# Gates of a hybrid block: one 512-column and one 256-column product a block in place of three of 256, and shorter pauses in the RWKV chain

## The chip, the cores and the metric

The kernel runs on one core of a Trainium2 chip. The metric is the device time of one execution in microseconds. Before the change the median of three runs is 1736.51 us (1735.34 to 1737.04).

The core has a matrix engine (PE, which loads weights, PEld in the profile, beside its matmuls), a vector engine (DVE), a scalar engine (ACT), GpSimd (POOL) and SyncE (SP), which here only issues DMAs. Each works through its own queue in order and waits on semaphores.

## The reference

One layer over 256 tokens of width 2048, in float32. The part that matters here is the first half: a projection gives the gates and the inputs of four branches (RG-LRU, attention with forgetting, SSD, RWKV-7); each branch's output goes through a matrix of its own, is multiplied by its gate, and the four are added.

```python
xn = rmsnorm(h, mix_norm[i])
proj = jnp.einsum('bsd,dn->bsn', xn, w_in[i])
(g_raw, a_x, a_g, b_q, b_k, b_v, b_f, c_z, c_xbc, c_dt, d_u) = jnp.split(proj, _offsets(IN_SPLIT), axis=-1)
...
gates = jax.nn.sigmoid(g_raw.astype(jnp.float32)).reshape(Bsz, S, N_BRANCH, D)
merged = gates[:, :, 0] * jnp.einsum('bsc,cd->bsd', branches[0], w_branch[i, 0])
for j in range(1, N_BRANCH):
    merged = merged + gates[:, :, j] * jnp.einsum('bsc,cd->bsd', branches[j], w_branch[i, j])
h = h + jnp.einsum('bsd,de->bse', merged, w_out[i]).astype(h.dtype)
...
# at the end of the RWKV branch
mean = jnp.mean(y, axis=-1, keepdims=True)
var = jnp.mean(jnp.square(y - mean), axis=-1, keepdims=True)
y = (y - mean) * lax.rsqrt(var + RWKV_LN_EPS) * ln_w.reshape(H, N) + ln_b.reshape(H, N)
```

A feed-forward part (2048 to 2 x 5632 and back) and a gated embedding follow; the change does not touch them.

## The kernel before

**Split products.** The weights are float32, and PE multiplies float32r. So each weight chunk of 512 KB (four blocks of 128 rows by 256 columns) comes in by one DMA on SP's queue into `wr`; `split` makes a high part of it on ACT (`wh`, a cast, line 214) and a low part on DVE (`wl = wr - wh`, line 215). There are three buffers each of `wh` and `wl`. The activations x are split in the same way into tiles of 512 columns: 256 tokens of the high part, then 256 of the low part. Each block is then the sum of three products: wh with the high x, wh with the low x, and wl with the high x.

**Two forms of a block.** `product` (line 242) does a block in two matmuls: `wh` with all 512 columns of x, so that a bank of PSUM holds the two sums side by side, and `wl` with the high 256 columns. The two halves of the bank are added afterwards by `joined` (line 254): a copy on ACT (line 256) and an add on DVE. Where x is handed over as a pair of halves (`halves`, and the tuple branch of `gemm_fm`), a block is three matmuls of 256 columns, all into the same half of the bank, and no `joined` is needed. The gates (`gate_unit`, line 1163) and the branch outputs (`branch_unit`, line 1171) have the second form; nearly all other projections, `w_out`, `w_up` and `w_down` have the first.

**The gate stage.** It goes branch by branch: a, c, b, d. For each branch there are 8 gate units; a unit is 256 output columns, two tiles (`m`) of 128, with K = 2048 in 16 blocks, four chunks. For the first three branches a branch unit (K = 512, one chunk, 24 matmuls) follows each gate unit; for the last (d, RWKV) the eight gate units run first, then `ready(3, "d")`, then the eight branch units. Units take their two banks of PSUM in turn from `psG`, which has four (`pg` in the profile).

**The four branches' own work** is written as Python generators (`lru`, `fox`, `ssd`, `rwkv`). `gemm_fm` calls a hook, `pump` (line 1091), after each tile of each chunk, and `pump` advances the oldest active generator by a step. So a `yield` in the generator is a place where projection work comes between two steps; `yield n` skips n hook calls, a time for a DMA to land. The chain of RWKV is the last: a triangular inverse by a recursion of 31 steps over `prod` and Q (a product on DVE, then a reduction, line 929), a round trip of the inverse through DRAM (`rw_q`, read into `qat` and `qbd`), `yield 9`, two sets of small products, four chunks of state, then centring with a matrix (`center`, four steps), squares with a mask matrix (`selR`, four steps of two products into `pr`, eight rows), a reciprocal, a square root and Newton steps, a round trip of the norm through DRAM (`rw_gn`), and the last multiplications.

**What sets the order.** Instructions are recorded in three lanes of priority: "g" (loads, splits, evacuations), "b" (the branches) and "m" (the projections' matmuls). A scheduler places each engine's instructions by priority and by its own estimate of when they are ready; a matmul of a branch takes the place of the projection's matmuls of that moment plus 16 (`on_pe`, line 130). On the chip each engine then keeps that order.

## Time and profile before

| | us |
|---|---|
| median of three runs (1735.34 to 1737.04) | 1736.51 |
| profiled execution | 1736.75 |
| its span | 1735.0 |

The span is the time from the first to the last instruction that the profile of this execution holds. The gates' weights are issued from 280.3 to 764.8 us; the feed-forward part follows. Lines that name `pg<-x,wh` and `pg<-x,wl` are projections, `pg<-sb,wh` and `pg<-sb,wl` branch outputs, `pb<-...` the branches' own products. A row of a group gives line, engine, operation, tiles, shapes and count, then busy time and mean duration in ns, then the idle time of the engine ahead of it and what ended it. In a timeline the columns are start, duration, engine, line, operation, tiles, with the wait ahead in brackets. A reader can find the chain, the groups and the waits quoted with the prediction.

### The profile page before, as it was taken

The page shows a single profiled execution, that of the slowest core. Times are in us where ns is not written, and L with a number is a line of the kernel's source. Part 1 is how long each engine was busy: PE and PEld are TensorE (multiplying, and loading weights), DVE is VectorE, ACT ScalarE, POOL GpSimd, SP SyncE. Part 2 cuts the span into 40 slices and gives each one's busy share as a digit, 9 for nine tenths or more (in the row PEclk, how much of TensorE's full clock was granted, in tenths as well). Part 3 has the DMA queues.
Part 4 walks back from the last instruction along what each step waited for, and adds up shares of the span by engine and source line. Part 5 has one row for each costly group of instructions (what it writes and reads, how often), then busy time and mean ns, then how long its engine had stood idle before and what let it go on. Part 6 is the DMA issues. An engine that isn't in the chain of part 4 may idle for free.

```text
span 1735.0 us, 29610 instructions
## 1 busy us (share of the span) xinstructions
PE 1716.0 (99%) x11555; PEld 1559.9 (90%) x11555; DVE 1232.9 (71%) x2002; ACT 948.8 (55%) x1428; POOL 92.8 (5%) x155
## 2 busy tenths in 40 slices
PE   9999999999999999999999999999999999999998
PEld 7888888999999999999888888888888888888887
DVE  6888768687789744648778777777777755555666
ACT  6677545556644444545556555555555544444554
POOL 1000000002320100000110000000000000000000
PEclk9999999999999999999999999999999999999999
DMA  9556556557775744565766656666566666666564
GB/s 328 170 170 203 177 172 220 184 181 209 207 214 172 262 153 149 175 187 182 250 212 191 192 187 191 189 189 192 186 191 201 211 207 189 195 192 186 174 224 134
DMA packets 99132, 338.36 MB, mean 195 GB/s; under 512 B 12362, under 2 KB 16624, under 8 KB 98736
## 3 DMA queue, kind: packets, MB, share of 16 engines
q1 hardware_dynamic: 90528, 310.94, 57.6%
q0 software_dynamic: 7456, 21.81, 4.2%
q10 hardware_dynamic: 1008, 3.73, 0.5%
q8 instruction: 90, 1.47, 0.3%
q14 instruction: 50, 0.41, 0.1%
HBM read 326.95 MB, written 9.48 MB: 194 GB/s over the span
## 4 chain that ended last, share of the span: by engine, by line
PE 89%; issue 8%; DMA 1%; DVE 1%; ACT 0%; POOL 0%; SPq 0%; DVEq 0%; POOLq 0%
PE pg L132 85%; PE pb L135 3%; PE pb L132 1%; DMA e<-ssd_ac 0%; DMA d<-in_xT_dram 0%; DVE wl L215 0%; DMA wr<-in_w_ax_dram 0%; DVE s L100 0%; DVE e L116 0%; ACT wh L214 0%; DMA ssd_ac<-sb 0%; DVE e L929 0%; DVE e L100 0%; SPq L382 0%; POOL prm L415 0%
## 5 line engine op out<-in xcount | busy, mean ns | idle before, releaser
L132 PE MATMUL pg<-x,wh 128*128 128x512 f32 (+1 forms) x4384 | 1173.4, 340 | 5.5 <-DVE sb L100 5.3
L215 DVE TENSOR_TENSOR wl<-wr,wh 128x1024 fp32r<-128x1024 f32 (+1 forms) x592 | 715.8, 1210 | 407.3 <-ACT wh L214 398.9
L214 ACT CAST wh<-wr 128x1024 fp32r<-128x1024 f32 (+1 forms) x592 | 615.2, 1041 | 646.4 <-PE pg L132 500.5
L132 PE MATMUL pg<-x,wl 128*128 128x256 f32 (+1 forms) x3344 | 919.2, 282 | 5.4 <-DVE wl L215 5.2
L132 PEld LDWEIGHTS pg<-x,wh 128*128 128x128 f32 x4384 | 748.7, 188 | 91.7 <-issue 3.2
L132 PEld LDWEIGHTS pg<-x,wl 128*128 128x128 f32 (+1 forms) x3344 | 629.6, 189 | 19.8 <-DVE wl L215 7.9
L132 PE MATMUL pg<-f,wh 128*128 128x512 f32 x704 | 243.2, 390 | 0.0
L132 PE MATMUL pg<-f,wl 128*128 128x256 f32 x704 | 195.8, 282 | 0.0
L132 PEld LDWEIGHTS pg<-f,wh 128*128 128x128 f32 x704 | 131.7, 188 | 26.9
L132 PEld LDWEIGHTS pg<-f,wl 128*128 128x128 f32 x704 | 133.0, 189 | 1.0
L132 PE MATMUL pg<-sb,wh 128*128 128x256 f32 x512 | 94.7, 283 | 0.0
L120 DVE SCALAR_TENSOR_TENSOR s<-s,prm 128x255 f32<-128x255 f32 (+1 forms) x176 | 84.2, 479 | 1.7 <-ACT s L127 1.0
L132 PEld LDWEIGHTS pg<-sb,wh 128*128 128x128 f32 x512 | 79.2, 188 | 0.1
L256 ACT COPY s<-pg 128x256 f32<-128x256 f32 x136 | 49.7, 366 | 44.7 <-PE pg L132 44.7
L132 PE MATMUL pg<-sb,wl 128*128 128x256 f32 x256 | 72.4, 284 | 0.0
L100 DVE TENSOR_TENSOR s<-s 128x256 f32<-128x256 f32 (+1 forms) x172 | 70.5, 420 | 1.3
L127 ACT ACTIVATE s<-s 128x256 f32<-128x256 f32 x140 | 56.6, 412 | 15.4 <-DVE s L100 15.0
L100 DVE TENSOR_TENSOR s<-s,pg 128x256 f32<-128x256 f32 x136 | 56.3, 415 | 9.4 <-ACT s L256 8.1
L127 ACT ACTIVATE s<-s,prm 128x256 f32<-128x256 f32 x88 | 52.5, 596 | 0.7 <-DVE s L100 0.7
L127 ACT ACT_TABLE_LOAD x40 | 51.3, 1283 | 2.2 <-PEq L1375 1.2
L132 PEld LDWEIGHTS pg<-sb,wl 128*128 128x128 f32 x256 | 48.0, 188 | 0.2
L132 PE MATMUL pg<-d,wh 128*128 128x512 f32 x128 | 45.2, 395 | 0.0
(235 smaller groups left out, 1154.0 us busy)
## 6 DMA issues: line engine op xcount, KB each, us to landing
wr<-in_w_up_dram SPq DMA_DIRECT2D x176, 512.0 KB, 4.3
wr<-in_w_g_dram SPq DMA_DIRECT2D x128, 512.0 KB, 3.9
wr<-in_w_down_dram SPq DMA_DIRECT2D x88, 512.0 KB, 4.3
wr<-in_w_p_dram SPq DMA_DIRECT2D x76, 512.0 KB, 3.8
wr<-in_w_branch_dram SPq DMA_DIRECT2D x32, 512.0 KB, 4.2
wr<-in_w_out_dram SPq DMA_DIRECT2D x32, 512.0 KB, 3.9
wr<-in_w_ple_gate_dram SPq DMA_DIRECT2D x32, 512.0 KB, 4.7
wr<-in_w_v_dram SPq DMA_DIRECT2D x8, 512.0 KB, 4.1
```

The costliest lines, as they stand in the source:

```text
L100: V.tensor_tensor(o, a, b, op=op)
L120: V.scalar_tensor_tensor(o, a, s, b, op0=op0, op1=op1)
L127: A.activation(o, i, f, **kw)
L132: return f(*a, **kw)
L135: f(*a, **kw)
L214: A.copy(wh, wr)
L215: V.tensor_tensor(wl, wr, wh.bitcast(F32), op=ALU.subtract)
L256: A.copy(o, pt[:, S:])
```

## The change

The gates' x is no longer cut into halves, so `gemm_fm` takes its first form there: per block one matmul of 512 and one of 256 columns instead of three of 256. Since the bank then holds two sums, the evacuation is `joined` (ACT copy, DVE add) and a multiplication by R in SBUF, where one multiplication out of PSUM stood before; the tanh on ACT stays. In the RWKV chain the pause behind the inverse's round trip is 5 hook calls instead of 9, and of the centring and of the squares the four steps each follow without a pause, with one pause behind them.

```diff
-        yield 9
+        yield 5
         px = bank()
...
             o = bslot()
             A.copy(o, pt[:, :S])
             yc.append(o)
-            yield
+        yield
         for j in range(4):
             s = bslot()
             act(s, yc[j], AF.Square)
             mm2(pr[:8, :S], selR[:, j], s, j == 0, j == 3, bp)
-            yield
+        yield
...
-    xg = [halves(x) for x in xs]
-
     def gate_unit(j, u, pool):
         def ev_g(m, pt):
             s = slot(pool=pool)
-            tt(s, pt[:, :S], R, ALU.mult)
+            joined(s, pt)
+            mul(s, s, R)
             act(s, s, AF.Tanh, scale=0.5)
             gates[2 * u + m] = s
-        gemm_fm(T["w_g"][8 * j + u], xg, ev_g)
+        gemm_fm(T["w_g"][8 * j + u], xs, ev_g)
```

The order of instructions changes on every engine from the first gate unit on. Three places at the end of the RWKV chain follow.

PE, the eight-row products of the squares (`pb_7866` before, `pb_7156` after; `exc` holds the mask and the centring matrix) among the gate products of branch d. Before, in one stretch of their run:

```order
L135 MATMUL pb_7866<-sb_7965,exc_387 8x256
L132 MATMUL pg_8194<-x_278,wl_8264 128x256
L132 MATMUL pg_8194<-x_281,wh_8263 128x256 x2
L132 MATMUL pg_8194<-x_281,wl_8264 128x256
L132 MATMUL pg_8195<-x_249,wh_8263 128x256 x2
L132 MATMUL pg_8195<-x_249,wl_8264 128x256
L132 MATMUL pg_8195<-x_252,wh_8263 128x256 x2
L132 MATMUL pg_8195<-x_252,wl_8264 128x256
L132 MATMUL pg_8195<-x_278,wh_8263 128x256
L135 MATMUL pb_7866<-sb_7966,exc_387 8x256
L135 MATMUL pb_7866<-sb_7985,exc_387 8x256
```

After, from behind the last product of branch d's gate unit 1 (`pg_7499`, `pg_7500`) to the first of unit 2 (`pg_7624`, which takes the bank of unit 0, `pg_7394`); `pb_7175` and `pb_7184` are centring:

```order
L135 MATMUL pb_7175<-sb_7177,exc_387 128x256
L135 MATMUL pb_7184<-sb_7185,exc_387 128x256
L135 MATMUL pb_7184<-sb_7186,exc_387 128x256
L135 MATMUL pb_7156<-sb_7207,exc_387 8x256
L135 MATMUL pb_7156<-sb_7208,exc_387 8x256
L135 MATMUL pb_7156<-sb_7215,exc_387 8x256
L135 MATMUL pb_7156<-sb_7216,exc_387 8x256
L135 MATMUL pb_7156<-sb_7223,exc_387 8x256
L135 MATMUL pb_7156<-sb_7224,exc_387 8x256
L135 MATMUL pb_7156<-sb_7231,exc_387 8x256
L135 MATMUL pb_7156<-sb_7232,exc_387 8x256
L132 MATMUL pg_7624<-x_119,wh_7628 128x512
```

The eight products, and three of the centring, now follow each other with no gate product between them.

DVE, the same place: splits (`wl`), the subtractions that make the squares' low parts (`sb_7208` to `sb_7232` after), the norm (`TENSOR_SCALAR` from `pb`, `RECIPROCAL`) and the evacuation of gate units. Before:

```order
L215 TENSOR_TENSOR wl_8368<-wr_8365,wh_8367 128x1024
L116 TENSOR_SCALAR sb_8070<-pb_7866 8x256
L124 RECIPROCAL sb_8071<-sb_8070 8x256
L215 TENSOR_TENSOR wl_8401<-wr_8398,wh_8400 128x1024
L100 TENSOR_TENSOR sb_8188<-pg_8049,R_104 128x256
L100 TENSOR_TENSOR sb_8191<-pg_8050,R_104 128x256
L100 TENSOR_TENSOR sb_8324<-pg_8194,R_104 128x256
L100 TENSOR_TENSOR sb_8327<-pg_8195,R_104 128x256
L100 TENSOR_TENSOR sb_8071<-sb_8069 8x256
L120 SCALAR_TENSOR_TENSOR sb_8071<-sb_8071,sb_8070 8x256
L120 SCALAR_TENSOR_TENSOR sb_8069<-sb_8071,sb_8069 8x256
L120 SCALAR_TENSOR_TENSOR sb_7874<-sb_7874,stamp_380,d_8080 128x256
```

After:

```order
L215 TENSOR_TENSOR wl_7673<-wr_7670,wh_7672 128x1024
L100 TENSOR_TENSOR sb_7186<-e_6426,sb_7185 128x256
L100 TENSOR_TENSOR sb_7208<-sb_7205,sb_7207 128x256
L100 TENSOR_TENSOR sb_7216<-sb_7213,sb_7215 128x256
L100 TENSOR_TENSOR sb_7224<-sb_7221,sb_7223 128x256
L100 TENSOR_TENSOR sb_7232<-sb_7229,sb_7231 128x256
L116 TENSOR_SCALAR sb_7280<-pb_7156 8x256
L124 RECIPROCAL sb_7281<-sb_7280 8x256
L100 TENSOR_TENSOR sb_7281<-sb_7279 8x256
L100 TENSOR_TENSOR sb_7489<-sb_7489,pg_7394 128x256
L120 SCALAR_TENSOR_TENSOR sb_7281<-sb_7281,sb_7280 8x256
L100 TENSOR_TENSOR sb_7494<-sb_7494,pg_7395 128x256
```

The split `wl_7673` is unit 2's third; its fourth, `wl_7695`, stands 23 rows further on, behind eight operations with the norm's copies out of DRAM (`d_7290`, `d_7291`), of which the first waits for a DMA. The evacuation of unit 0 stands behind the reciprocal.

DVE once more, a little later after the change: unit 3's second and third splits (`wl_7751`, `wl_7773`) and the evacuations of unit 1 (`pg_7499`, `pg_7500`), whose banks unit 3 takes, and of unit 2.

```order
L215 TENSOR_TENSOR wl_7751<-wr_7748,wh_7750 128x1024
L100 TENSOR_TENSOR sb_7191<-sb_7191,sb_4953 128x256
L215 TENSOR_TENSOR wl_7773<-wr_7770,wh_7772 128x1024
L100 TENSOR_TENSOR sb_7607<-sb_7182,sb_7606 128x256
L100 TENSOR_TENSOR sb_7611<-sb_7191,sb_7610 128x256
L100 TENSOR_TENSOR sb_7614<-sb_7614,pg_7499 128x256
L100 TENSOR_TENSOR sb_7619<-sb_7619,pg_7500 128x256
L100 TENSOR_TENSOR sb_7714<-sb_7714,pg_7624 128x256
L100 TENSOR_TENSOR sb_7719<-sb_7719,pg_7625 128x256
```

The evacuation of unit 1 stands behind unit 3's third split, whose buffer is the one of unit 2's fourth chunk three splits earlier.

## The prediction

> **What bounds the kernel now.** First the share of each engine and the chain of work that ended last, both from the page.

> ```profile
> PE 1716.0 (99%) x11555; PEld 1559.9 (90%) x11555; DVE 1232.9 (71%) x2002; ACT 948.8 (55%) x1428; POOL 92.8 (5%) x155
> PE 89%; issue 8%; DMA 1%; DVE 1%; ACT 0%; POOL 0%; SPq 0%; DVEq 0%; POOLq 0%
> ```

> PE sets the end: a matmul taken away shortens the kernel, and a stretch in which PE stands still lengthens it by its own length. So two things have to be priced: PE's pace in the gates, and PE's waits. From the list of who waited for whom, the waits of PE:

> ```profile
> PE pg L132 <- DVE sb L100: 5.3, 3, 2.9
> PE pg L132 <- DVE wl L215: 5.2, 4, 2.5
> PE pg L132 <- DVE s L100: 0.2, 1, 0.2
> ```

> They are few. The longest on a gate is in the timeline of PE at 708 us, with the same stretch by windows (columns: length; busy us and instructions of PE, PEld, DVE, ACT, POOL; granted clock; DMA share; GB/s):

> ```profile
> 708.35 0.27 PE L132 MATMUL pg<-x,wl 128*128 128x256 f32 x1
> 711.49 0.80 PE L132 MATMUL pg<-x,wh 128*128 128x256 f32 x2 [2.87 <-DVE sb L100]
> 708.40:711.50 3.10, 0.23 (x3) 0.03 (x2) 3.10 (x4) 2.90 (x4) 0.00 (x0) 0.86 0.54 169
> 711.50:718.30 6.80, 6.80 (x35) 6.80 (x36) 2.09 (x6) 2.77 (x6) 2.96 (x5) 0.56 0.35 110
> 718.30:725.00 6.70, 6.70 (x59) 6.70 (x59) 5.44 (x11) 3.18 (x5) 1.13 (x3) 1.00 0.64 171
> ```

> From 708.35 to 711.49 PE starts nothing: 3.1 us. Then its clock is granted at 0.56 for 6.8 us, and it starts 35 products where the next 6.7 us hold 59, one in 0.114 us: 6.8 - 35 x 0.114 = **2.8 us** lost to the clock. This one place, the end of the RWKV chain, costs 5.9 us. DVE, at the same place, shows why:

> ```profile
> 706.35 1.23 DVE L215 TENSOR_TENSOR wl<-wr,wh 128x1024 fp32r<-128x1024 f32 x1 [1.39 <-ACT wh L214]
> 707.85 0.41 DVE L116 TENSOR_SCALAR sb<-pb 8x256 f32<-8x256 f32 x1 [0.27 <-PE pb L135]
> 708.29 1.74 DVE L124 RECIPROCAL sb<-sb 8x256 f32<-8x256 f32 x1
> 709.96 1.15 DVE L215 TENSOR_TENSOR wl<-wr,wh 128x1024 fp32r<-128x1024 f32 x1
> 711.04 1.39 DVE L100 TENSOR_TENSOR sb<-pg,R 128x256 f32<-128x256 f32 x4
> 712.36 0.40 DVE L100 TENSOR_TENSOR sb<-sb 8x256 f32<-8x256 f32 x1
> 712.80 0.86 DVE L120 SCALAR_TENSOR_TENSOR sb<-sb 8x256 f32<-8x256 f32 x2
> 719.56 0.88 DVE L120 SCALAR_TENSOR_TENSOR sb<-sb,stamp,d 128x256 f32<-128x256 f32 x2 [5.90 <-DMA d<-rw_gn]
> ```

> The four evacuations at 711.04 free PE's banks. They stand in DVE's queue behind a reciprocal and a split (`wl`), so PE waits though its operands are there. Later DVE itself stands 5.90 us for a round trip through DRAM (`rw_gn`).

> **Term 1, the gates' matmuls.** From the chain: a stretch of gates and branches, and one of 512+256 pairs.

> ```profile
> 488.97 67.11 PE pg L132 x569
> 1642.63 11.11 PE pg L132 x64
> ```

> 67.11/569 = 0.118 us a product, so three are 0.354 us; 11.11/32 = 0.347 us a pair. That is 0.007 us a block. The gates have 32 units x 16 x 2 = 1024 blocks: **-7.0 us**. The third matmul is nearly all given back, because the 512-column one streams as many columns as the two that it replaces. [...]

> **Term 2, the evacuation.** Before, one DVE pass; after, an ACT copy, a DVE add and a DVE multiply, whose durations stand in the groups of other stages:

> ```profile
> L100 DVE TENSOR_TENSOR s<-pg,R 128x256 f32<-128x256 f32 x48 | 19.9, 421 | 12.7 <-PE pg L132 12.6
> L256 ACT COPY s<-pg 128x256 f32<-128x256 f32 x136 | 49.7, 366 | 44.7 <-PE pg L132 44.7
> L100 DVE TENSOR_TENSOR s<-s,pg 128x256 f32<-128x256 f32 x136 | 56.3, 415 | 9.4 <-ACT s L256 8.1
> 480.00:520.00 40.00, 40.00 (x343) 40.00 (x342) 32.46 (x68) 18.05 (x25) 8.32 (x13) 1.00 0.78 222
> 520.00:540.00 20.00, 20.00 (x171) 20.00 (x171) 19.71 (x31) 8.73 (x11) 0.00 (x0) 1.00 0.57 176
> 540.00:580.00 40.00, 39.81 (x336) 39.55 (x336) 39.93 (x48) 16.12 (x18) 0.00 (x0) 1.00 0.55 172
> ```

> A tile costs 0.37 us more on ACT and about 0.33 more on DVE (0.42, of which a neighbour overlaps some). ACT has room. DVE has room nearly everywhere (32.46 of 40 us), but from 520 to 580 us it is busy 59.6 of 60, with the recursion over `prod` and Q. A gate unit with its branch unit takes 32 x 0.354 + 24 x 0.118 = 14.2 us, so some 4.2 units with two tiles each fall there: 4.2 x 2 x 0.33 = **+2.8 us**. The ends are 0 (PE never waits in that stretch today, so there is some stock) and 6 (a copy and an add per tile, 0.79 us, late at eight tiles).

> **Term 3, the shortened pauses.** Four hook calls less at `yield 9` take 4 x 12 x 0.118 = 5.7 us out of the time between the last `rw_q` write and the products that read `qat`.

> ```profile
> 591.94 1.29 POOL L940 DMA_DIRECT2D qat<-rw_q x2 [0.51 <-DMA rw_q<-e]
> DMA to landing us min/median/max: 6.4/6.6/6.8
> 607.09 0.30 PE L135 MATMUL pb<-qat,ltb 64*64 64x32 f32 x2
> ```

> The second of the two is issued at 592.6 and lands by 599.4, 7.7 us ahead of its reader; 2.0 us stay. I take 0; if POOL's queue is late, up to 3 us of wait, in the upper end. The gates' 512-column products stand behind it in PE's queue.

> The two yields moved out of their loops cost more. PE's order shows the four centring steps and the eight 8-row products no longer spread among gate products, but the last three of the former and all the latter in one block. What ACT does there has these durations today:

> ```profile
> 698.57 0.37 ACT L1034 COPY sb<-pb 128x256 f32<-128x256 f32 x1 [1.43 <-PE pb L135]
> 700.11 0.40 ACT L221 CAST sb<-sb 128x256 fp32r<-128x256 f32 x1
> 700.42 0.41 ACT L127 ACTIVATE sb<-sb 128x256 f32<-128x256 f32 x1
> 700.86 0.41 ACT L221 CAST sb<-sb 128x256 fp32r<-128x256 f32 x1
> 701.18 0.41 ACT L127 ACTIVATE sb<-sb 128x256 f32<-128x256 f32 x1
> 708.55 1.04 ACT L214 CAST wh<-wr 128x1024 fp32r<-128x1024 f32 x1 [2.23 <-PE pg L132]
> 710.90 0.41 ACT L127 ACTIVATE sb<-sb 8x256 f32<-8x256 f32 x1
> ```

> Let PE finish the last gate product of unit 1 (units are counted among the last branch's eight) at T0.

> - (A) That product frees a `wh` buffer (three of them), so ACT's cast starts at T0: 1.05; DVE's split 1.23, and behind it the subtraction of the fourth centring step, 0.42; product 0.28; copy 0.37. Then four squares with their casts, 0.76 a pair (700.42 to 701.18): 3.0; last subtraction 0.42, product 0.28. Sum 7.1.
> - (B) The next gate product needs unit 0's bank, whose add stands behind this norm's reciprocal: scalar op 0.41, reciprocal 1.74, square root 0.41, ACT's copy 0.37, add 0.42: 3.4. With A and some ten handovers of 0.04: 10.9 us, of which 11 small products at 0.118 are work: **9.6 us idle**.
> - (C) Unit 2 then has three chunks: 24 pairs, 8.3 us. Its fourth split stands in DVE's queue behind the reads of `rw_gn`: six small steps 2.2, the wait 5.9, eight passes at 0.40 (0.88 for two) 3.2, split 1.23: 12.5 after the square root, which is 0.8 ahead of PE's start. **3.4 us**, or as much of it as the lower clock stretches the three chunks.
> - (D) Unit 3 needs unit 1's banks; their adds stand behind a split whose buffer only unit 2's last chunk frees: cast 1.05, split 1.23, two subtractions 0.66, add 0.42, handovers 0.1: **3.5 us**. It is today's wait of 3.1 us once more.
> - (E) Clock: after A and B it will surely fall, but that loss and C cover each other. After D, by the nearest row (3.1 us idle, then 0.56), **2.8 us** once more; ends 0 and 5.6.

> A to E give 19.3 us and the 5.9 of today go with the old order: **+13.4 us**. [...]

> **Sum.** The profiled execution took 1736.75 us (span 1735.0), 0.24 above the median of 1736.51. 1736.75 - 7.0 + 2.8 + 13.4 = 1745.9; from the median **1745.7**.

> **Rivals.**

> - The tail is half covered: PE's 9.6 us let ACT and DVE split ahead, C and D vanish, as nothing waited after 711 us today although DVE stood 5.9 us; the clock falls once. 1745.7 - 3.4 - 3.5 = 1738.8, and without term 2 1736.0: no change. Against it: three buffers a kind hold no more than three chunks, and D hangs on a bank. 0.18.
> - Faster: as above, and the small products keep the clock up, and A's steps overlap by 0.08 at twenty places (1.6 us). Then 1736.5 - 7.0 + 8.0 - 5.9 = 1731.6. It decides where the tail's idle time stays under 12.9 us (5.9 + 7.0). For it: neighbours on ACT do overlap (700.11, 700.42). Against: the reciprocal and the eight products form one chain, with nothing of PE's to fill it. 0.12.
> - [...] 0.20.
> - The change doesn't do what it says: a pair in the gates takes three products' time, because its weights load no faster. Term 1 goes: 1752.7. Against it stand the 32 pairs at 0.347. 0.05.

> The forecast has 0.45.

> **Numbers.** 0.2% (3.5 us) is about what a measurement of this kernel tells from no change. Slower 0.45 + 0.20 + 0.05 = 0.70; within 0.18; faster 0.12. The range leaves out the faster rival and some of the top: 1734 to 1753; term 2 at 6 and a `qat` wait of 3 would give 1751.9, the fourth rival 1752.7.

> **What would show it.** Right: 2048 products of gates instead of 3072, 0.347 us a pair in undisturbed stretches; near 715 us an idle stretch of PE broken only by 8-row products, then two waits, for `wl` and for an add out of `pg`; a granted clock near 0.5 there; DVE still full around 540 to 580 with short waits of PE. Wrong: gates at another pace, or PE busy through the RWKV end; then the time falls below 1735. A wait for `qat` would put it above 1748.

## The result and the profile after

| | before | after |
|---|---|---|
| median of four runs, us | 1735.92 (1735.01 to 1737.04) | **1752.92** (1751.39 to 1754.01) |
| profiled execution, us | 1736.75 | 1753.18 |
| its span, us | 1735.0 | 1751.4 |

The ratio is 1.0091, 95% interval 1.0079 to 1.0102: slower by 17 us, where 9.2 were forecast (1745.7). It lies inside the predicted range of 1734 to 1753 by less than 0.1 us, and two of the four times lie above 1753: that the range held is luck. The page of the changed kernel, first the engines, then the chain that ended last:

```profile
PE 1718.1 (98%) x10531; PEld 1513.5 (86%) x10531; DVE 1254.7 (72%) x2066; ACT 969.6 (55%) x1492; POOL 92.5 (5%) x155
PE 68%; issue 9%; DVE 4%; DMA 2%; POOL 1%; ACT 0%; POOLq 0%; DVEq 0%
```

1024 matmuls are gone, yet PE is busy 2 us longer, and its share of the chain fell from 89% to 68%. A busy PE is not a fast PE here: at the lower clock fewer products fill the same busy time (12 the 3.41 us from 724.28 at a granted clock of 0.50, 22 the 3.41 us from 727.69 at 1.00). The waits of PE name the rest:

```profile
PE pg L132 <- DVE sb L100: 9.6, 4, 3.6
PE pg L132 <- DVE wl L215: 8.6, 11, 2.5
PE pb L135 <- ACT sb L221: 4.4, 3, 1.6
```

The pace of the gates did improve. In PE's timeline of an undisturbed unit of branch d, its first pair and, 32 pairs on, the first of the next unit:

```profile
759.72 0.39 PE L132 MATMUL pg<-x,wh 128*128 128x512 f32 x1
770.83 0.39 PE L132 MATMUL pg<-x,wh 128*128 128x512 f32 x1
```

And before, the same stretch, two `wl` products that lie 96 products apart:

```profile
748.05 0.28 PE L132 MATMUL pg<-x,wl 128*128 128x256 f32 x1
759.36 0.28 PE L132 MATMUL pg<-x,wl 128*128 128x256 f32 x1
```

So a unit takes 11.11 us (0.347 a pair) in place of 11.31. Gate and branch unit of the first three branches take 14.00 in place of 14.19 where nothing disturbs them. About 0.195 x 32 units = **6.2 us** are gained.

They are lost several times over at the end of the RWKV chain. PE's rows that waited there, and three windows:

```profile
711.51 0.28 PE L135 MATMUL pb<-sb,exc 128*128 128x256 f32 x1
713.38 0.38 PE L135 MATMUL pb<-sb,exc 128*128 128x256 f32 x1 [1.59 <-ACT sb L221]
714.40 0.58 PE L135 MATMUL pb<-sb,exc 128*128 128x256 f32 x1 [0.64 <-DVE sb L100]
716.20 3.11 PE L135 MATMUL pb<-sb,exc 128*8 128x256 f32 x8 [1.21 <-ACT sb L221]
722.90 0.76 PE L132 MATMUL pg<-x,wh 128*128 128x512 f32 x1 [3.60 <-DVE sb L100]
734.65 0.39 PE L132 MATMUL pg<-x,wl 128*128 128x256 f32 x1 [0.97 <-DVE wl L215]
741.27 0.70 PE L132 MATMUL pg<-x,wh 128*128 128x512 f32 x1 [3.58 <-DVE sb L100]
```

```profile
711.50:723.00 11.50, 4.14 (x13) 1.30 (x11) 6.41 (x11) 7.58 (x17) 0.00 (x0) 0.61 0.33 91
723.00:728.00 5.00, 5.00 (x17) 4.28 (x18) 1.43 (x5) 1.62 (x3) 2.24 (x4) 0.53 0.05 11
737.00:745.00 8.00, 4.42 (x16) 3.56 (x16) 6.46 (x15) 4.22 (x11) 0.00 (x0) 0.79 0.68 220
```

From 711.51 to 722.90 PE starts eleven small products and nothing else: 11.4 us, some 10.1 of them lost. The clock is at half until 728 (granted 0.50 from 714.04 to 727.69; 2.2 us lost), then come a wait for `wl` (1.2), one for a bank (3.7) and the lower clock once more (0.50 from 741.34 to 744.76; 1.6). Together 18.8 us where it was 5.9: **+12.9 to +13.0**.

Waits came up in places that the prediction passed over. Near 417 us, DVE's row with the same operation before, where nothing waited, and then DVE's and ACT's rows after:

```profile
407.01 0.48 DVE L120 SCALAR_TENSOR_TENSOR sb<-sb,stamp,d 128x256 f32<-128x256 f32 x1
```

```profile
416.74 0.48 DVE L120 SCALAR_TENSOR_TENSOR sb<-sb,stamp,d 128x256 f32<-128x256 f32 x1 [4.18 <-DMA d<-rw_kn]
418.00 1.22 DVE L215 TENSOR_TENSOR wl<-wr,wh 128x1024 fp32r<-128x1024 f32 x1
419.87 0.41 DVE L100 TENSOR_TENSOR s<-s,pg 128x256 f32<-128x256 f32 x1
```

```profile
417.78 0.41 ACT L221 CAST sb<-sb 128x256 fp32r<-128x256 f32 x1 [3.99 <-DVE sb L120]
418.09 0.37 ACT L256 COPY s<-pg 128x256 f32<-128x256 f32 x1
```

DVE stands 4.18 us at a round trip through DRAM (`rw_kn`); behind it in the queues stand a split, ACT's copy of a gate tile and the add that frees the bank. PE starts nothing for 1.8 and 1.0 us at 416 to 420, and then runs at half clock for 3.4 (granted 0.50 from 420.49 to 423.90). Together some 4.3 us are lost there.

A second place is the round trip of `fox_rn` near 300 us, DVE's and PE's row after:

```profile
297.74 1.67 DVE L120 SCALAR_TENSOR_TENSOR sb<-sb,gain,e 128x256 f32<-128x256 f32 x4 [2.81 <-DMA e<-fox_rn]
302.12 0.39 PE L132 MATMUL pg<-x,wl 128*128 128x256 f32 x1 [1.00 <-DVE wl L215]
```

Some 2.0 us are lost there, and no gate tile has been evacuated in the new form yet. Of the kernels below, b_y5_d8, with the old gates, has the same wait of 1.00 us at 301.79, and gates_y5, with the new ones, has none. So the added passes are not needed for it.

To sum up by stage, the **gate stage** is taken here from the start of the first `wl` product of the gates to that of the last branch product, both from PE's rows (before 293.95 to 805.01, after 294.31 to 821.41): 511.1 and 527.1 us. What follows it lasts the same in every kernel of this study (923.4 us to the last matmul), and what precedes it scatters from run to run, so this stage is compared below. The branches share its +16.0 as +4.1 (a), +1.3 (c), -3.9 (b) and +14.5 (d). With 1.55 a branch for the pace, a and c lost 5.6 and 2.9 to waits, 6.3 of these at the two places above; the other 2.2 were not traced. Some 65 small products of RWKV moved from b to d, about 3 us of work; that leaves 0.7 of waits in b and the 13.0 of the tail in d. -6.2 + 9.2 + 13.0 = 16.0.

### The profile page after: what moved, and what is told of

It is laid out like the page before. It is cut to its first block, busy times and chain, and to the rows that moved or that the text cites. A ratio compares the mean times of both kernels' runs of the same rounds, so it can differ in the third digit from the quotient of the medians.

```text
span 1751.4 us, 27647 instructions
## 1 busy us (share of the span) xinstructions
PE 1718.1 (98%) x10531; PEld 1513.5 (86%) x10531; DVE 1254.7 (72%) x2066; ACT 969.6 (55%) x1492; POOL 92.5 (5%) x155
## 4 chain that ended last, share of the span: by engine, by line
PE 68%; issue 9%; DVE 4%; DMA 2%; POOL 1%; ACT 0%; POOLq 0%; DVEq 0%
PE pg L132 66%; DVE wl L215 1%; PE pb L135 1%; DVE e L100 1%; PE pb L132 1%; DVE s L100 1%; DMA e<-fox_rn 1%; DVE e L929 1%; DVE sb L120 0%; DMA d<-rw_kn 0%; DMA rw_q<-e 0%; DMA d<-rw_gn 0%; ACT wh L214 0%; DVE sb L114 0%; DVE sb L100 0%
## 5 line engine op out<-in xcount | busy, mean ns | idle before, releaser
L132 PE MATMUL pg<-x,wh 128*128 128x512 f32 (+1 forms) x3360 | 1166.4, 393 | 10.7 <-DVE sb L100 9.6
L215 DVE TENSOR_TENSOR wl<-wr,wh 128x1024 fp32r<-128x1024 f32 (+1 forms) x592 | 715.6, 1210 | 402.2 <-ACT wh L214 396.1
L214 ACT CAST wh<-wr 128x1024 fp32r<-128x1024 f32 (+1 forms) x592 | 615.4, 1041 | 615.0 <-PE pg L132 495.5
L132 PE MATMUL pg<-x,wl 128*128 128x256 f32 (+1 forms) x3344 | 913.7, 283 | 8.6 <-DVE wl L215 8.6
L132 PEld LDWEIGHTS pg<-x,wh 128*128 128x128 f32 (+1 forms) x3360 | 624.5, 188 | 132.3 <-issue 10.5
L132 PEld LDWEIGHTS pg<-x,wl 128*128 128x128 f32 (+1 forms) x3344 | 632.5, 189 | 29.3 <-DVE wl L215 12.6
L132 PE MATMUL pg<-f,wh 128*128 128x512 f32 x704 | 243.2, 390 | 0.0
L132 PE MATMUL pg<-f,wl 128*128 128x256 f32 x704 | 195.8, 282 | 0.0
L132 PEld LDWEIGHTS pg<-f,wh 128*128 128x128 f32 x704 | 131.7, 188 | 26.9
L132 PEld LDWEIGHTS pg<-f,wl 128*128 128x128 f32 x704 | 133.0, 189 | 1.0
L256 ACT COPY s<-pg 128x256 f32<-128x256 f32 x184 | 67.4, 367 | 65.5 <-PE pg L132 65.3
L132 PE MATMUL pg<-sb,wh 128*128 128x256 f32 x512 | 95.2, 284 | 0.0
L100 DVE TENSOR_TENSOR s<-s,pg 128x256 f32<-128x256 f32 x184 | 75.9, 414 | 14.2 <-ACT s L256 12.9
L120 DVE SCALAR_TENSOR_TENSOR s<-s,prm 128x255 f32<-128x255 f32 (+1 forms) x176 | 84.0, 477 | 1.7 <-ACT s L127 1.0
L132 PEld LDWEIGHTS pg<-sb,wh 128*128 128x128 f32 x512 | 80.7, 188 | 1.4
L100 DVE TENSOR_TENSOR s<-s 128x256 f32<-128x256 f32 (+1 forms) x172 | 70.5, 420 | 1.4
L132 PE MATMUL pg<-sb,wl 128*128 128x256 f32 x256 | 71.4, 283 | 0.0
L127 ACT ACTIVATE s<-s 128x256 f32<-128x256 f32 x140 | 57.1, 413 | 16.1 <-DVE s L100 15.6
L100 DVE TENSOR_TENSOR s<-s,R 128x256 f32<-128x256 f32 x152 | 63.6, 421 | 2.1
L127 ACT ACTIVATE s<-s,prm 128x256 f32<-128x256 f32 x88 | 52.5, 596 | 0.7 <-DVE s L100 0.7
L132 PEld LDWEIGHTS pg<-sb,wl 128*128 128x128 f32 x256 | 48.0, 189 | 0.1
```

What stands on the lines that cost most here:

```text
L100: V.tensor_tensor(o, a, b, op=op)
L120: V.scalar_tensor_tensor(o, a, s, b, op0=op0, op1=op1)
L127: A.activation(o, i, f, **kw)
L132: return f(*a, **kw)
L214: A.copy(wh, wr)
L215: V.tensor_tensor(wl, wr, wh.bitcast(F32), op=ALU.subtract)
```

## The experiments

Each kernel was timed beside the kernel before. The last four columns are from its profiled execution: the length of the gate stage; how long after the stage's start the last step of the RWKV chain's recursion (last L929 row of DVE) and its reciprocal (L124, eight rows) begin; and the longest wait of PE in the tail (after 690 us). A stage is that of one execution, and it has its own scatter. In seven kernels (after, gates_only, after_no_join, g_y5_d8, b_y5_d8, gates_acb, gates_part) DVE stands 1.6 us or more at `fox_rn`, and PE's wait near 300 us costs up to 2.4 us; in the others DVE stands 1.3 us or less there or not at all, or g_y5_r60 passes it earlier, and PE doesn't wait. Before was timed in four series; its medians are given as a span.

| kernel | median us | ratio (95%) | stage | recursion | reciprocal | tail wait |
|---|---|---|---|---|---|---|
| before | 1735.9 to 1737.4 | 1 | 511.1 | 287.0 | 414.3 | 2.9 |
| after | 1752.92 | 1.0091 [1.0079, 1.0102] | 527.1 | 301.7 | 425.5 | 3.6 |
| gates_only | 1744.45 | 1.0035 [1.0020, 1.0049] | 520.2 | 301.6 | 425.3 | 3.6 |
| yields_only | 1742.52 | 1.0031 [1.0020, 1.0041] | 514.8 | 286.9 | 408.3 | 8.5 |
| y5_only | 1732.19 | 0.9971 [0.9959, 0.9983] | 504.3 | 286.9 | 408.3 | none |
| after_no_join | 1744.17 | 1.0038 [1.0023, 1.0053] | 516.7 | 289.7 | 415.7 | 4.7 |
| gates_y5 | 1746.67 | 1.0057 [1.0042, 1.0072] | 520.5 | 301.3 | 424.9 | 3.6 |
| g_y5_d8 | 1743.20 | 1.0045 [1.0028, 1.0062] | 516.1 | 295.7 | 420.7 | 3.6 |
| g_y5_r60 | 1742.01 | 1.0028 [1.0018, 1.0038] | 505.3 | 236.6 | 344.8 | none |
| b_y5_d8 | 1732.57 | 0.9974 [0.9965, 0.9983] | 508.3 | 288.0 | 406.9 | 1.7 |
| gates_b | 1737.47 | 1.0003 [0.9994, 1.0012] | 510.5 | 288.2 | 414.5 | 3.2 |
| gates_d | 1737.05 | 0.9998 [0.9989, 1.0007] | 508.3 | 286.9 | 410.6 | 1.4 |
| gates_acb | 1742.65 | 1.0029 [1.0018, 1.0040] | 514.9 | 300.7 | 420.7 | 2.6 |
| gates_part | 1732.42 | 0.9973 [0.9963, 0.9984] | 505.0 | 294.2 | 408.8 | none |

### The parts of the change

**gates_only**: the gates' part of the change, all yields as before.

```diff
-    xg = [halves(x) for x in xs]
...
-            tt(s, pt[:, :S], R, ALU.mult)
+            joined(s, pt)
+            mul(s, s, R)
...
-        gemm_fm(T["w_g"][8 * j + u], xg, ev_g)
+        gemm_fm(T["w_g"][8 * j + u], xs, ev_g)
```

> Only the gates' part of the change; the RWKV chain's pauses as before. Theory 1 (the prediction's: the two moved yields make the block of small products at the RWKV end): no idle block there, PE's waits of the earlier gates stay, 1736 - 7.7 + 11 = 1739 to 1740 us. Theory 2 (the block comes from the gates' new form, because the chain's end is recorded in one go by the final drain whatever its yields say; PE's order of this kernel shows the block already): idle block of about 11 us near 715 us, no wait of 3.5 us before the unit after next: 1747 to 1750 us.

Measured: 1744.45, between the two theories' times. PE's rows of the tail:

```profile
711.55 0.39 PE L135 MATMUL pb<-sb,exc 128*128 128x256 f32 x1 [1.59 <-ACT sb L221]
712.57 0.39 PE L135 MATMUL pb<-sb,exc 128*128 128x256 f32 x1 [0.63 <-DVE sb L100]
714.16 0.28 PE L135 MATMUL pb<-sb,exc 128*8 128x256 f32 x1 [1.21 <-ACT sb L221]
720.87 0.76 PE L132 MATMUL pg<-x,wh 128*128 128x512 f32 x1 [3.60 <-DVE sb L100]
```

The block stands here as in the changed kernel, wait for wait, without a moved yield: it is the second theory's block, in 2.6 us less than that theory's least. Why its last wait is 3.6 us is seen on ACT:

```profile
715.97 0.40 ACT L221 CAST sb<-sb 128x256 fp32r<-128x256 f32 x1
716.39 1.28 ACT L127 ACT_TABLE_LOAD   x1
719.53 0.41 ACT L127 ACTIVATE sb<-sb 8x256 f32<-8x256 f32 x1 [1.85 <-DVE sb L124]
719.85 1.14 ACT L256 COPY sb<-pg 128x256 f32<-128x256 f32 x4
```

The copies of four gate tiles, which the new form needs before a bank is free, stand behind the squares' casts, a table load and the square root, which itself waits for the reciprocal. The later wait (741.27 in the changed kernel) is missing: that one belongs to the moved yields.

**yields_only** has the pause of 5 and the two moved yields, with the old gates; **y5_only** has the pause of 5 alone.

```diff
-        yield 9
+        yield 5
```

> Only the RWKV part of the change; the gates in three products as before. Theory 1: the idle block of A and B stands at the RWKV end, 1736 + 13 = 1749 us. Theory 2: no block; its order has one evacuation behind a split at the RWKV end, a wait of 4 to 5 us with the clock lowered once, in place of today's 3.1 us with the same: 1736 to 1739 us.

> Only yield 9 to 5. Prediction's term 3: nothing, 1736 us. Theory 2: the chain's end moves against the gates, and the order no longer has an evacuation behind a split there; today's 5.9 us go: 1730 to 1732 us. If qat lands late: over 1737.

Measured: 1742.52 and 1732.19. The shorter pause alone makes the kernel **faster**, by 0.29%, 0.2 us above its second theory's range. None of PE's waits lies in the tail any more; the two largest sums left, all from before 690 us:

```profile
PE pg L132 <- DVE wl L215: 5.7, 4, 2.8
PE pg L132 <- DVE sb L100: 2.4, 2, 1.5
```

The table says how: the recursion ends where it did (286.9), and the reciprocal comes 6.0 us earlier against the gates, behind 129 of DVE's splits in place of 131 (rows of L215, counted from 8 us ahead of the stage), where PE has other work; the 5.9 us of before are gone. With the moved yields the time lies between its theories, 1736 to 1739 and 1749 us: there is no block, but a longer wait than either had. The reciprocal comes as early as with the pause alone, and PE then stands longer than in any other kernel. DVE and then PE:

```profile
717.70 0.88 DVE L120 SCALAR_TENSOR_TENSOR sb<-sb,stamp,d 128x256 f32<-128x256 f32 x2 [2.75 <-DMA d<-rw_gn]
722.24 0.88 DVE L120 SCALAR_TENSOR_TENSOR sb<-sb,stamp,d 128x256 f32<-128x256 f32 x2 [1.74 <-DMA d<-rw_gn]
729.01 1.41 DVE L100 TENSOR_TENSOR sb<-pg,R 128x256 f32<-128x256 f32 x4
```

```profile
720.79 0.28 PE L132 MATMUL pg<-x,wl 128*128 128x256 f32 x1
729.57 0.77 PE L132 MATMUL pg<-x,wh 128*128 128x256 f32 x2 [8.50 <-DVE sb L100]
```

In y5_only two of these four evacuations stand at 709 us, ahead of the reads of `rw_gn`; here all four stand behind them, and PE waits 8.5 us for their banks.

**after_no_join**: the changed kernel, with the gates evacuated by the old single pass. It leaves the product of `wh` with the low part of x out of the gates' sums; PE still makes it.

```diff
-            joined(s, pt)
-            mul(s, s, R)
+            tt(s, pt[:, :S], R, ALU.mult)
```

> The changed kernel, but the gates' evacuation is the old single multiplication out of PSUM: it leaves out the sum of wh with the low x in the gates. If the copy, the add and the order that they bring cause the waits of the earlier gates (at 299, 416 to 424 and 577 to 595 us, some 11 us): those go, the RWKV end stays bad: 1740 to 1745 us. If PE's shorter units alone cause them: 1751 us or more.

Measured: 1744.17, as the first case had it. The waits of 416 to 424 us are gone, but 0.96 us near 300 and 0.95 us at 585 remain. The recursion's last step begins at 289.7 in place of 301.7: the two further passes are most of what makes the chain late. The tail is not healed:

```profile
713.62 0.77 PE L132 MATMUL pg<-x,wh 128*128 128x512 f32 x1 [2.65 <-DVE sb L100]
732.34 0.73 PE L132 MATMUL pg<-x,wh 128*128 128x512 f32 x1 [4.71 <-DVE sb L100]
```

The second is the wait of the moved yields again.

### Is it the yields, or the order?

Four kernels with all yields in their loops and the pause of 5: **gates_y5** with the new gates; **g_y5_d8** the same with DELAY 8; **g_y5_r60** the same with RATE 0.6; **b_y5_d8** the old gates with DELAY 8. DELAY is the number of places that a branch's matmul is put back (16 before). RATE is the credit that each hook call gives the branches' generators, which pay for their steps out of it (0.5 before): more of it records the branches' work earlier.

```diff
-DELAY, RATE, STEP = 16, 0.5, 0.2
+DELAY, RATE, STEP = 16, 0.6, 0.2
```

> The changed kernel with the two moved yields put back into their loops; gates' new form and the pause of 5 stay. Theory 1 (the block of waits at the RWKV chain's end comes from the new gates alone, and the moved yields add the last long wait, for an add out of pg, with its half clock): the block of about 11 us stays, the later wait of 4 us and the half clock behind it go, 1743 to 1746 us. Theory 2 (a shorter pause is worth as much here as alone, 4.7 us): gates alone took 1744.5, so 1739 to 1741 us and no block. Theory 3 (the moved yields cost nothing): as the changed kernel, 1751 to 1754 us.

> As gates_y5 with 8 products of cover in place of 16. Theory 1 (the chain's end comes earlier against the projections, so the gates' saving shows): below 1738 us. Theory 2 (the block stays, as the order of unit 1 and the eight products does not depend on the cover): 1742 to 1748 us. Theory 3 (cover is needed): 1750 us or more.

> As gates_y5, and the planner's RATE is 0.6 in place of 0.5, which places the branches' chain against the projections otherwise. Theory 1 (the gates' 7.7 us are real and are given back only where PE meets the chain's end and DVE's round trips in an unlucky order): another order of the same work takes most of the waits away, 1728 to 1738 us. Theory 2 (two more passes of DVE and ACT a tile make the chain late in whatever order): 1742 to 1754 us, with a block of small products again.

> The old gates and yields, the pause of 5, and the branches' matmuls put 8 products behind the projections' place in place of 16. Theory 1 (PE loses only where a branch's product has its operands late; with the pause of 5 no such wait is left at the RWKV end, so 8 places more or less move little): 1730 to 1734 us. Theory 2 (16 products are the cover that handovers of 2 us need; with 8, each product of a chain makes PE wait some 0.9 us): 1750 us or more.

gates_y5 took 1746.67, just above its first theory's range: the block is there, the later wait is not. So the moved yields cost 6.6 us of stage beside the new gates (527.1 - 520.5; 6.2 by the medians). And the pause, worth 6.8 us of stage alone, is worth nothing beside the new gates (520.2 against 520.5): with them the recursion's last step comes 14.4 us later (301.3 against 286.9), and in both kernels it and the reciprocal stand behind the same number of DVE's splits, 99 and 132. Why the shorter pause doesn't move them there was not tested.

g_y5_d8 keeps the block (516.1; its second theory). b_y5_d8 is as fast as y5_only by the median, though its profiled execution has a stage 4.0 us longer, with a wait of 1.7 us in the tail and the one near 300 us: less cover gained nothing.

g_y5_r60 is the telling miss. Its stage is 505.3 us with **all** gates in the new form: where the chain runs ahead (recursion at 236.6) there is no block. But the higher rate holds before the gates too, and there it costs: the gates start at 302.9 us in place of 294. PE's row:

```profile
100.83 0.76 PE L132 MATMUL pg<-x,wh 128*128 128x512 f32 x1 [3.67 <-DVE sb L100]
```

After it the granted clock falls (0.97 from 100 to 200 us, some 6 us of it at half). Theory 1 was right on the stage and wrong on the sum, 1742.0 in place of 1728 to 1738. The number is theory 2's lowest, but theory 2's block isn't there.

### Which gates make the chain late

The pause of 5, and the new form in some gates only, by a condition in `gate_unit`: **gates_b** `j == 1`, **gates_d** `j == 3`, **gates_acb** `j < 3`, **gates_part** as below.

```diff
+        pair = (j == 0 and u < 4) or (j == 2) or (j == 3 and u > 3)
+
...
+            if pair:
+                joined(s, pt)
+                mul(s, s, R)
+            else:
+                tt(s, pt[:, :S], R, ALU.mult)
...
+        gemm_fm(T["w_g"][8 * j + u], xs if pair else xg, ev_g)
```

> Pause of 5, and the new form in the gates of branch b alone (256 of 1024 blocks); the RWKV end, in the gates of d, has the old form. The pause of 5 alone took 4.7 us off. Theory 1 (the tail's waits come back because the new evacuations slow DVE in its full stretch of 520 to 605 us, and the RWKV chain on DVE reaches its end later against PE): the pace takes 1.8 us off, waits of about 2 us at 575 to 600 us, and near 720 us PE waits 3 to 9 us again for an add out of pg although the gates there are of the old form; 1735 to 1739 us. Theory 2 (the tail's block is made by the copies and adds of d's own gates): no wait of over 1 us after 610 us, 1730 to 1733 us.

> Pause of 5, and the new form in the gates of branch d alone, the ones that lie beside the RWKV end. Theory 1 (a late chain makes the block): the chain is not late here, so at most short waits after 700 us, no half clock, 1730 to 1734 us. Theory 2 (d's own copies and adds make it): the block of 11 us and the half clock near 715 us, 1741 to 1746 us.

> Pause of 5, and the new form in the gates of branches a, c and b; d's have the old form. Theory 1: the waits of 410 to 425 and 575 to 600 us and a tail with waits of 4 us or more near 720 us, less than the whole block since d's evacuation is one pass: 1736 to 1743 us. Theory 2: the waits of 410 to 425 and 575 to 600 us (5 and 2 us) alone, against 5.3 us of pace: 1732 to 1735 us, no wait in the tail.

> Pause of 5, and the new form only where neither DVE is full nor the chain's end lies: the first four units of a, all of c, the last four of d (512 of 1024 blocks). Theory 1 (there the pace is kept and no new wait comes): 3.5 us off the pause of 5 alone, less 1 us of short waits: 1728 to 1731 us, faster than both kernels. Theory 2 (each tile's two further passes cost PE something wherever they lie): 1732 us or more.

The recursion's last row on DVE: in the kernel before, in the changed kernel, in gates_acb.

```profile
580.93 1.19 DVE L929 TENSOR_REDUCE e<-e 64x31 f32<-64x961 f32 x1
```

```profile
595.98 1.17 DVE L929 TENSOR_REDUCE e<-e 64x31 f32<-64x961 f32 x1
```

```profile
596.61 1.14 DVE L929 TENSOR_REDUCE e<-e 64x31 f32<-64x961 f32 x1
```

Less the start of their stages (293.95, 294.31, 295.89), these are the 287.0, 301.7 and 300.7 of the table. Ahead of this last step DVE evacuates 38 tiles in the new form in the last two, 24 in gates_part and 4 in gates_b, and the step comes 14.7, 13.7, 7.2 and 1.2 us later than before: **0.30 to 0.39 us a tile**. DVE's busy time of the whole kernel gives the same price: (1254.7 - 1232.9)/64 tiles = 0.34. So the whole price shows in the chain, although DVE is 71% busy.

How it gets there is shown for gates_b alone. There the last step stands behind 96 of DVE's splits, as before, so its 1.2 us are delay on a full DVE (busy 59.00 of 60 us from 530 to 590). In gates_part it stands behind 98 splits, in the changed kernel and gates_acb behind 99: two or three chunks of the gates, of 2.8 us each, that the recorded order now puts first. And of the changed kernel's 14.7 us, 7.7 are there when the recursion begins (217.2 in place of 209.5), ahead of the stretch in which DVE is full. What of this is the passes' time, what the order's move and what the waits near 300 and 417 us was not separated.

gates_b met its first theory: 1737.47, and the wait of the kernel before is back, in gates of the old form:

```profile
711.15 0.80 PE L132 MATMUL pg<-x,wh 128*128 128x256 f32 x2 [3.21 <-DVE sb L100]
```

It takes the whole worth of the pause away. Only 1.2 us of it are the recursion's; the reciprocal comes 6.2 us later than in y5_only, about where it stood before. That is the order: it stands behind 131 of DVE's splits again, in place of 129, and PE has started 17 more `wl` products by then (1024 in place of 1007), which with their `wh` products are 17 x 0.354 = 6.0 us. Why four tiles move the order so is not settled here. gates_d has no block and no half clock in its profiled run (1734.14, mean granted clock 1.000), but short waits in the tail:

```profile
709.11 0.47 PE L132 MATMUL pg<-x,wh 128*128 128x512 f32 x1 [0.96 <-DVE sb L100]
727.39 0.39 PE L132 MATMUL pg<-x,wl 128*128 128x256 f32 x1 [1.36 <-DVE wl L215]
734.81 0.48 PE L132 MATMUL pg<-x,wh 128*128 128x512 f32 x1 [1.39 <-DVE sb L100]
```

Beside y5_only its stage is 4.0 us longer, where the pace could have given 1.6 us; the median, 1737.05, lies between the two theories' ranges, and the profiled run is the fastest of its eleven. gates_acb went as theory 1 had it in time, 1742.65; its tail has several waits, of 2.6 us at the most where theory 1 had 4. Beside the pause of 5, the new form costs 10.6 us of stage in a, c and b (some 2.4 of it at the wait near 300 us), 4.0 in d, and 16.2 in all four. PE's order shows the late chain too: branch d holds 80 of the branches' small products in the changed kernel, gates_only, gates_y5 and gates_acb, and 12 to 16 in before, y5_only, gates_b, gates_d and gates_part. So neither theory holds alone: most of the block needs the late chain, and d's own copies and adds make it longer.

gates_part, 1732.42, missed theory 1's 1728 to 1731 and came out as theory 2 had it. Beside y5_only its stage is 0.7 us longer, not 3.5 shorter; without the wait near 300 us, some 1.6 us that y5_only didn't have, it would be 0.9 shorter. In branch c the three units that nothing disturbs take 14.00 in place of 14.19; the five in which another branch's products run give nothing together. Half of the gates in the new form are no gain over the pause alone. y5_only, with one number changed, stays the best version; gates_part and b_y5_d8 are as fast within their intervals.

## Why the prediction was right, and where it was not

The time fell within the range, at its very end, and the forecast was the right case, 7 us too low. Step by step:

- **Term 1** (-7.0 forecast) was right in kind and nearly in size: -6.2.
- **Term 2** (+2.8, at most 6) is the step that failed: +9.2. Its rows were right, 0.33 us more of DVE a tile against 0.34 measured; the place was wrong. In branch b, where DVE is full with the recursion (busy 59.08 of 60 us from 520 to 580), the waits grew by a mere 0.7 us. Everywhere else the prediction put the loss at nothing, since "DVE has room nearly everywhere", read from busy shares; there, in branches a and c, 8.5 us were lost. Some 4.3 of them fell where DVE stands at a round trip (`rw_kn` near 417 us) with a copy, a split and an add queued behind it. Another 2.0 fell at `fox_rn` near 300 us, a wait that b_y5_d8 has with the old gates too, so the term's passes are not needed for it; the remaining 2.2 were not traced. The busy share doesn't show such places; the waits of DVE for a DMA do.
- **The tail** (+13.4) measured +13.0, almost term by term: A and B 10.1 lost (9.6 forecast), C with the clock 3.4 (3.4), D 3.7 (3.5), E 1.6 (2.8). But the cause named was wrong. The prediction put the block down to the moved yields, which gates_y5 shows to be false: the new gates alone make it, mostly since the chain is late (gates_d, without the late chain, has only short waits, and g_y5_r60, with an early one, has none). To the moved yields belongs D, with its clock. The size came out because it was worked out from the changed order, whatever had caused that.
- **Term 3** (0) holds in the changed kernel: no wait of PE there is for `qat`. Taken as the worth of that edit, it is wrong: the pause alone takes 0.29% off. The prediction asked only whether `qat` would be late, not what comes earlier if the chain does.
- **The sum**: term 2 was 6.4 too low, term 1 0.8 too good, the tail 0.4 too high, and the stage started 0.4 later: 7.2, the distance of the measured span (1751.4) from the forecast one (1744.2).
- **The rivals**: a tail half covered did not come about (C and D are both there), nor did PE stay busy through the chain's end, nor did the clock stay up after D. That it would, 0.20 of the chances, no run shows: behind D's wait of 3.58 us the changed kernel's clock was granted at 0.50 from 741.34 to 744.76 us. The fourth rival's 1752.7 is the number nearest to the measured one, but its mechanism is not there: a pair takes 0.347 us.

## What to carry to other kernels

Where a chain of another engine runs beside PE, an added pass on that engine can be priced twice: as its share of busy time, and as a delay of the chain. Here the chain came 0.30 us a tile later where the order stayed as it was, and up to 0.39 where the order moved too, with the engine 71% busy. Try the parts of a change apart: here one number of it made the kernel 0.29% faster and the rest took more than that back. And when a step of the order is read from the changed program, its size may hold where its cause does not: here the same block appeared without the edit that seemed to make it.

## What the runs showed of the hardware

PE did not stand still for all of the 3.41 us ahead of a fall: it was busy 42% of them before (from 707.19), and 44, 45 and 2% after (from 417.08, 710.62 and 737.93; the last is D's wait). At 162 us it was busy 52% of 3.41 us before (from 161.06) and 58% after (from 161.08), and the clock stayed at 1.00. In the four quarters of the 13.65 us after, PE was busy 49, 50, 40 and 100%, so eleven small products in 11.4 us (711.5 to 723) did not bring the clock back; in the two halves of the 6.83 us before it was busy 74 and 100%. These are shares of the profile's busy time, whose matmul ends are modelled.

The length of a wait alone does not tell whether the clock falls. With the 2.87 us of before (to 711.49) and the 3.21 us of gates_b (to 711.15) it fell: it was granted at 0.50 from 710.61 to 717.43 in the one, and the `wl` product at 711.75 took 0.41 us in place of 0.28 in the other. With the 3.09 us of b_y5_d8 (to 165.66) it did not: it was granted at 1.00 from 100 to 200 us. What else decides was not shown.

One place scatters from run to run. At 162 us, before the gates, DVE waits for a round trip (`ssd_ac`), and a split that PE needs stands behind it. In gates_part's profiled execution:

```profile
161.65 1.66 DVE L116 TENSOR_SCALAR e<-e,ssd_col 128x128 f32<-128x128 f32 x8 [3.48 <-DMA e<-ssd_ac]
165.66 1.22 DVE L215 TENSOR_TENSOR wl<-wr,wh 128x1024 fp32r<-128x1024 f32 x1
```

```profile
166.93 0.58 PE L132 MATMUL pg<-x,wl 128*128 128x256 f32 x1 [4.44 <-DVE wl L215]
```

PE waited 4.44 us there, and 2.34 in gates_b, whose program is the same up to that point. After the longer wait the granted clock fell: it is 0.96 from 100 to 180 us, and 1.00 in gates_b. The place lies ahead of the gates, which is why the stage, and not the whole time, is compared above. How much of the scatter of the times it accounts for was not tested.
